# Strassen down-projection for blocks 0 to 15 of the first feed-forward group, with its weight sums split between attention and GpSimd

## The chip, the cores and the metric

The kernel runs on one core of one Trainium2 chip. The metric is the device time of one execution in microseconds; the figure given is the median of three runs. A core has TensorE (PE; its weight loads are listed apart as PEld), VectorE (DVE), ScalarE (ACT), GpSimd (POOL) and SyncE (SP), which here only issues DMAs. Each engine works off its own queue in order and waits on semaphores.

## What is computed

One step of a streaming encoder layer over 2048 prompt tokens and 64 sample tokens (2112 in all), model width 1024, in float32:

```
h  = rmsnorm(x, g1) * (1 + sc1) + sh1          # sc, sh, gt from c @ w_ada
u, q, k, v, o, gates = split(h @ w_in)
mix = concat(pool_mixer(u), mlstm(q, k, v, gates) * sigmoid(o)) @ w_out
x  = x + gt1 * mix
h2 = rmsnorm(x, g2) * (1 + sc2) + sh2
up = h2 @ w_up                                  # 1024 -> 2 * 2816
a, g = split(causal depthwise conv of width 3 over up)
x  = x + gt2 * ((silu(g) * a) @ w_down)         # 2816 -> 1024
y  = rmsnorm(x, g_final)
```

and the states of the pool, the mLSTM and the convolution.

## The kernel before, in words

**Precision.** Every large matmul is done in three passes of `F32R` operands: high x high, high x low, low x high. A weight tile ("unit", 128 x 512) is loaded by SP, ScalarE writes its rounded high part (line 428) and VectorE subtracts that from it for the low part (line 431). `stream` lists all units in the order of use; `pump` loads ahead of use, six or seven units deep.

**Stages.** Attention runs over four groups of 512 tokens (the last has 576). The feed-forward part then runs over three groups of 704 tokens, two column halves of 352 each, and 22 blocks of 128 gated features. `PARTS` (line 33) cuts the blocks of each group into parts. In a part, each block's up-projection (`Pair.products`, line 1720) is done in Strassen's form (Winograd's variant): seven products of 12 matmuls, with sums of the weights (`wsum`, made during attention) and sums of the activations (`Bo`: the seven operands B11, B21, T1 to T4 and B22). Two results make the a and g halves, which go through the convolution, silu and gate.

**The down projection** of a part comes in two forms. *Plain* (`down`, matmuls at line 2230): for each of eight rows of 128 outputs, all blocks of the part, in columns 0 to 448 and 448 to 704; 24 x 2 matmuls per block. *Strassen* (`quad_down`, matmuls at line 2084), for parts of exactly four blocks (`paired`, line 39): the four gated blocks are split into seven operands by `step_2` to `step_7` (ScalarE the high parts, VectorE the low parts and the differences `less`, line 1831), and two `duo`s of 14 half products each, of six matmuls of 352 columns, are added to the rows `x` (line 2053). A quad is held back and done after the first block of the next part. It needs 14 weight units: raw quarters from `w_quad` and sums from `dsum`, eight sets `d` of four matrices, two sets to a quad. `dsum` is made by `quad_sums` (line 1666) in 16 pieces, each a load, four VectorE operations of 128 x 256 and a store.

Before the change, groups two and three have `(0,4) (4,8) (8,12) (12,16) (16,22)`: four quads and one plain part. The first group has `(0,6) (6,12) (12,16) (16,22)`: one quad and three plain parts, because `dsum` is made only while it runs.

**Side work and its order.** In the feed-forward part PE, ACT, DVE and POOL run in the order of the program text. Side work is written as generators in five queues `bg`; `tick(i)` runs the next step of queue i at marked places of the main work, and `drain` runs a queue to its end on the spot. `bg[0]` is ticked twice in each product, `bg[1]` four times a block and after every fourth half product of a quad. `bg[4]` is ticked in attention's projections (line 485), not while `quiet` is set. `quad_sums` runs from `bg[0]` in the first feed-forward group. Ahead of blocks 12 to 15 there, `drain(0)` finishes it and `bg[1]` is set aside.

`prepare` (line 840) makes the next group's `Bo` in the background of `bg[1]`: it normalises rows (line 750), then `sums_of` with `slow=True` makes seven operands for each of four row pairs: ScalarE a high part (line 809), VectorE the low part (line 795) and the sums (line 791), ScalarE's queue the store to `Bd`. `up_sums` (line 874) makes `wsum` in attention: 44 pieces of two loads, four VectorE operations of 128 x 256 (lines 898 to 903) and a store, on `bg[4]` from attention's second group on.

GpSimd's queue in the feed-forward part holds the halo copies of the convolution (`ext_tile`, `conv_scale`, lines 1572 and 1586) and, in the last part of a group, additions of squares (line 2045).

Of the kernel before, what the change touches and what calls it, by code (L numbers as in the profile page):

```python
# [16 lines left out]
P = 128  # L17
# [7 lines left out]
NF = 22  # L25
# [41 lines left out]
def tile_layer(ctx: ExitStack, tc: tile.TileContext, xT, vecs, cst, rst, w_mod, w_ada, w_qkou, w_v, w_pool,  # L67
# [716 lines left out]
    def sums_of(xs, put, slow=False, pin=lambda d: d):  # L784

        H = FH
# [3 lines left out]
        def minus(out, a, b):  # L790
            pin(dve.tensor_tensor(out=out, in0=a, in1=b, op=ALU.subtract))

        def low():
            for nm, src, hi, lo, end in late:
                pin(dve.tensor_tensor(out=lo, in0=src, in1=hi.bitcast(F32), op=ALU.subtract))
# [71 lines left out]
    if True:  # L867
# [6 lines left out]
        def up_sums():  # L874

            def load(f, c):
                w = a1.tile([P, 4, 256], F32, tag="w4", name="w4", bufs=4)
                for i in range(2):
                    tc.keep_in_program_order(nc.sync.dma_start(out=w[:, 2 * i:2 * i + 2, :], in_=w_up[NF * i + f].rearrange(
                        "p (h c) -> p h c", h=2)[:, :, c:c + 256]))  # L880
                return w
            todo = [(f, c) for f in range(NF) for c in (0, 256)]
# [3 lines left out]
            def store():  # L886
                if made:
                    f, c, w = made.pop()
                    pin(nc.sync.dma_start(out=wsum[f, :, :, c:c + 256], in_=w))
# [582 lines left out]
        for o in groups:  # L1472
            drain(1)
            if o.g == 1:
                bg[4].append(up_sums())
# [55 lines left out]
            quiet.append(1)  # L1531
            mix[:NH] = [mx_tile(gi, o) for gi in range(NH)]
# [133 lines left out]
    def quad_sums(ds):  # L1666

        for d in ds:
            for c in (0, 256):
                t = f2.tile([P, 2, FT], F32R, tag="av", name="qs", bufs=AVB)  # L1670
                w = t.bitcast(F32).rearrange("p a t -> p (a t)")[:, :1024].rearrange("p (i c) -> p i c", i=4)
                nc.sync.dma_start(out=w, in_=w_quad[d, :, :, c:c + 256])
                for _ in range(7):
                    yield
                a11, a12, a21, a22 = (w[:, i] for i in range(4))
                dve.tensor_tensor(out=a22, in0=a21, in1=a22, op=ALU.add)
                yield
                dve.tensor_tensor(out=a21, in0=a11, in1=a21, op=ALU.subtract)
                yield
                dve.tensor_tensor(out=a11, in0=a22, in1=a11, op=ALU.subtract)  # L1680
                yield
                dve.tensor_tensor(out=a12, in0=a12, in1=a11, op=ALU.subtract)
                yield
                yield
                nc.sync.dma_start(out=dsum[d, :, :, c:c + 256], in_=w)
                yield
                yield

# [20 lines left out]
    class Pair:  # L1709
# [121 lines left out]
        def less(self, out, a, b):  # L1831
            dve.tensor_tensor(out=out, in0=a, in1=b, op=ALU.subtract)
# [223 lines left out]
    def quad_down(o, quad, cur, done, last=False):  # L2056
# [7 lines left out]
        def duo(d):  # L2064
            units, banks = {}, {}

            def half_product(nm, role, X, op, first=False):
# [20 lines left out]
                tick(1 if len(count) % 4 == 0 else 0)  # L2088
# [74 lines left out]
    for o in fgroups:  # L2163
        Bo = B[o.g]
        held = None
        for pi, part in enumerate(PARTS[o.g]):
# [224 lines left out]
```

## Time and profile before

| what | value |
|---|---|
| median of three runs | 2168.61 us (2168.05 to 2170.31) |
| span of the profiled execution | 2165.8 us |
| PE, DVE, ACT, POOL busy | 2143.9, 1649.8, 1105.2, 265.3 us |
| attention, to the first up-product | 787.1 us |
| first feed-forward group: to its last plain part; that part | 414.7; 47.7 us |
| second group, the same | 405.5; 47.8 us |
| third group, to its last plain part | 401.9 us |

The profile is one execution, taken by the hardware profiler. A row of a window gives its bounds and length, the busy time and the instructions of PE, PEld, DVE, ACT and POOL, the granted TensorE clock, the share of the DMA engines and GB/s. A row of a group gives line, engine, operation, output and inputs with their shapes, the count, then busy time, mean duration in ns, and the idle time of the engine ahead of it with what ended most of that. A row of the timeline or of the chain begins with start and length in us. Busy matmuls are pipelined, so PE's busy time says that it had work, not that it ran at its peak.

### The profile page before, as it was taken

The page shows a single profiled execution, that of the slowest core. Times are in us where ns is not written, and L with a number is a line of the kernel's source. Part 1 is how long each engine was busy: PE and PEld are TensorE (multiplying, and loading weights), DVE is VectorE, ACT ScalarE, POOL GpSimd, SP SyncE. Part 2 cuts the span into 40 slices and gives each one's busy share as a digit, 9 for nine tenths or more (in the row PEclk, how much of TensorE's full clock was granted, in tenths as well). Part 3 has the DMA queues.
Part 4 walks back from the last instruction along what each step waited for, and adds up shares of the span by engine and source line. Part 5 has one row for each costly group of instructions (what it writes and reads, how often), then busy time and mean ns, then how long its engine had stood idle before and what let it go on. Part 6 is the DMA issues. An engine that isn't in the chain of part 4 may idle for free.

```text
span 2165.8 us, 38050 instructions
## 1 busy us (share of the span) xinstructions
PE 2143.9 (99%) x13529; PEld 2038.3 (94%) x13529; DVE 1649.8 (76%) x3060; ACT 1105.2 (51%) x2193; POOL 265.3 (12%) x475
## 2 busy tenths in 40 slices
PE   8999999999999999999999999999999999999998
PEld 7888888888899999999999999999999999999998
DVE  5777679677675778788688768988877597887874
ACT  4554335234333557465556445655655365565554
POOL 0010000001000301010001220100101321111112
PEclk9999999999999999999999999999999999999999
DMA  8987997897799689797768976665668675555542
GB/s 320 331 304 225 325 311 249 292 325 259 247 294 296 207 273 317 241 343 248 229 219 305 360 282 207 228 225 202 219 234 276 221 251 190 171 175 188 172 159 76
DMA packets 297063, 541.09 MB, mean 250 GB/s; under 512 B 25728, under 2 KB 113280, under 8 KB 296872
## 3 DMA queue, kind: packets, MB, share of 16 engines
q1 hardware_dynamic: 286280, 513.44, 70.3%
q10 hardware_dynamic: 10592, 25.20, 3.0%
q8 instruction: 107, 1.75, 0.3%
q14 instruction: 84, 0.69, 0.1%
HBM read 412.56 MB, written 125.98 MB: 249 GB/s over the span
## 4 chain that ended last, share of the span: by engine, by line
PE 89%; DVE 4%; DMA 3%; issue 1%; ACT 1%; SPq 0%; POOL 0%; POOLq 0%; DVEq 0%; ACTq 0%
PE mm L1616 37%; PE mm L495 23%; PE mm L2230 11%; PE mm L2084 10%; PE mm L1155 3%; DVE wt L431 1%; PE m L1345 1%; PE m L1365 1%; PE m L1367 1%; PE m L1330 1%; DMA wt<-dsum 0%; PE mm L1091 0%; DMA qs<-w_quad 0%; DVE tg L1594 0%; DMA raw<-w_up 0%
## 5 line engine op out<-in xcount | busy, mean ns | idle before, releaser
L1616 PE MATMUL mm<-hx,wt 128*128 128x352 f32 x5544 | 886.1, 321 | 2.5 <-DVE wt L431 2.2
L1616 PEld LDWEIGHTS mm<-hx,wt 128*128 128x128 f32 x5544 | 878.3, 188 | 4.9 <-DVE wt L431 4.2
L495 PE MATMUL mm<-hl,wt 128*128 128x512 f32 (+2 forms) x1920 | 385.4, 356 | 0.0
L431 DVE TENSOR_TENSOR wt<-raw,wt 128x512 fp32r<-128x512 f32 (+1 forms) x460 | 310.8, 681 | 79.1 <-ACT wt L428 77.7
L428 ACT ACTIVATE wt<-raw 128x512 fp32r<-128x512 f32 (+1 forms) x460 | 274.7, 604 | 168.0 <-PE mm L495 53.2
L495 PEld LDWEIGHTS mm<-hl,wt 128*128 128x128 f32 x1920 | 314.7, 188 | 47.4 <-issue 4.4
L2084 PE MATMUL mm<-av,wt 128*128 128x352 f32 x1512 | 248.0, 323 | 1.7 <-DVE x L2053 0.7
L2084 PEld LDWEIGHTS mm<-av,wt 128*128 128x128 f32 x1512 | 242.3, 188 | 4.8 <-DVE ea L1625 2.8
L2230 PE MATMUL mm<-av,wt 128*128 128x448 f32 (+1 forms) x1440 | 231.4, 322 | 0.0
L2053 DVE SCALAR_TENSOR_TENSOR x<-mm,MOD,x 128x352 f32<-128x352 f32 (+3 forms) x368 | 171.9, 507 | 77.8 <-PE mm L2230 62.0
L2230 PEld LDWEIGHTS mm<-av,wt 128*128 128x128 f32 x1440 | 220.8, 188 | 9.7
L1664 ACT ACTIVATE mm<-mm 128x352 f32<-128x352 f32 x204 | 91.4, 448 | 238.9 <-PE mm L1616 175.1
L495 PE MATMUL mm<-mx,wt 128*128 128x512 f32 (+1 forms) x960 | 182.6, 352 | 0.0
L495 PEld LDWEIGHTS mm<-mx,wt 128*128 128x128 f32 x960 | 159.3, 188 | 22.5
L1594 DVE SCALAR_TENSOR_TENSOR ta<-ea,V,ta 128x704 f32<-128x704 f32 (+1 forms) x132 | 125.7, 953 | 60.4 <-ACT ta L1589 56.3
L1594 DVE SCALAR_TENSOR_TENSOR tg<-eg,V,tg 128x704 f32<-128x704 f32 (+1 forms) x132 | 125.7, 952 | 49.8 <-ACT tg L1589 47.2
L431 DVE TENSOR_TENSOR wt<-wt 128x512 fp32r<-128x512 f32 x204 | 138.7, 685 | 10.9 <-ACT wt L428 10.7
L428 ACT ACTIVATE wt<-wt 128x512 fp32r<-128x512 f32 x204 | 123.8, 622 | 25.9 <-DMA wt<-wsum 24.7
L1572 POOL COPY ea<-UC 128x2 f32<-128x2 f32 x66 | 35.0, 530 | 529.1 <-DVE ta L1594 418.4
L1812 ACT ACTIVATE tg<-tg 128x704 f32<-128x704 f32 (+1 forms) x66 | 52.5, 796 | 71.3 <-DVE tg L1594 71.3
L1155 PE MATMUL mm<-wt,hl 128*128 128x256 f32 (+1 forms) x576 | 71.2, 284 | 0.0
L1155 PEld LDWEIGHTS mm<-wt,hl 128*128 128x128 f32 x576 | 70.3, 189 | 0.8 <-issue 0.6
(305 smaller groups left out, 2222.7 us busy)
## 6 DMA issues: line engine op xcount, KB each, us to landing
wt<-wsplit SPq DMA_DIRECT2D x132, 512.0 KB, 4.2
raw<-w_up SPq DMA_DIRECT2D x198, 256.0 KB, 4.1
wt<-hl_kept SPq DMA_DIRECT2D x96, 512.0 KB, 5.9
wt<-wsum SPq DMA_DIRECT2D x132, 256.0 KB, 4.9
wsplit<-wt SPq DMA_DIRECT2D x66, 512.0 KB, 5.3
w<-w_up SPq DMA_DIRECT2D x88, 256.0 KB, 4.7
wsum<-w SPq DMA_DIRECT2D x44, 512.0 KB, 5.3
Bd<-fscr ACTq DMA_DIRECT2D x56, 352.0 KB, 3.4
```

The lines of the kernel that those rows point to most:

```text
L428: act.activation(u.w[:, 0, :u.n], u.raw[:, :u.n], AF.Copy)
L431: dve.tensor_tensor(out=u.w[:, 1, :u.n], in0=u.raw[:, :u.n], in1=u.w[:, 0, :u.n].bitcast(F32), op=ALU.subtract)
L495: pe.matmul(ps[bi][:, :hi - lo], U[:, a, k % 4 * P:(k % 4 + 1) * P], mv[k][:, b, lo:hi], start=(at == 0 and pi == 0), stop=(k == order[-1] ...
L1155: pe.matmul(ps[ti][:n, :cols], h[4 * kh + k4][:, b, lo:lo + n], U[:, a, k4 % 2 * cols:(k4 % 2 + 1) * cols], start=(kh == 0 and k4 == 0 and ...
L1572: pool.tensor_copy(ext[:, 0:2], UC[:, f, :])
L1594: dve.scalar_tensor_tensor(out=t[:, :E], in0=ext[:, j:j + E], scalar=wc(j, f), in1=t[:, :E], op0=ALU.mult, op1=ALU.add)
L1616: pe.matmul(bk.t[:, :FH], U[:, a, kc * P:(kc + 1) * P], Bo.at(nm, kc, b), start=(first and kc == 0 and pi == 0), stop=(kc == 3 and pi == 2 ...
L1664: act.activation(to.t[:, :FH], bk.t[:, :FH], AF.Copy)
L1812: act.activation(self.tg[:, :E], self.tg[:, :E], AF.Silu)
L2053: dve.scalar_tensor_tensor(out=x3[n][:, a:b], in0=bk.t[:, a - lo:b - lo], scalar=gt2(n, s), in1=x3[n][:, a:b], op0=ALU.mult, op1=ALU.add)
L2084: pe.matmul(bk.t[:, :FH], U[:, a, c:c + P], quad.put(op, m, b), start=(first and m == 0 and pi == 0), stop=(m == 1 and pi == 2), skip_grou ...
L2230: pe.matmul(bks[i].t[:, :hi - lo], U[:, a, k % 4 * P:(k % 4 + 1) * P], av[k][:, b, lo:hi], start=(k == 0 and (a, b) == PASSES[0]), stop=(k ...
```

## The change

- `PARTS`: the first group gets the parts of the other two, so quads 0 to 2 are added and two plain parts of six blocks go. The drain and the set-aside queue ahead of blocks 12 to 15 go.
- `up_sums` becomes `weight_sums`: after the 44 pieces it makes eight more, of `dsum` sets 0 to 3. It is put on `bg[4]` in the first attention group, ahead of its pooling projections, and takes a piece in 3.5 steps where it took four.
- `quad_sums` makes the other eight pieces (sets 4 to 7), with GpSimd in place of VectorE, in scratch tiles of their own, on `bg[1]` from the first block on, ahead of `prepare`.
- `sums_of(slow=True)`, so `prepare` for groups two and three, makes its low parts and sums on GpSimd.
- `less` is on GpSimd in the first group.
- In the first group a quad ticks `bg[1]` after every third half product.

```diff
-PARTS = (((0, 6), (6, 12), (12, 16), (16, 22)), ((0, 4), (4, 8), (8, 12), (12, 16), (16, 22)),
+PARTS = (((0, 4), (4, 8), (8, 12), (12, 16), (16, 22)), ((0, 4), (4, 8), (8, 12), (12, 16), (16, 22)),
-SUMS = ((6, 7, 0, 1, 2), (3, 4, 5))
...
     def sums_of(xs, put, slow=False, pin=lambda d: d):
+        eng = pool if slow else dve
...
-            pin(dve.tensor_tensor(out=out, in0=a, in1=b, op=ALU.subtract))
+            pin(eng.tensor_tensor(out=out, in0=a, in1=b, op=ALU.subtract))
...
-                pin(dve.tensor_tensor(out=lo, in0=src, in1=hi.bitcast(F32), op=ALU.subtract))
+                pin(eng.tensor_tensor(out=lo, in0=src, in1=hi.bitcast(F32), op=ALU.subtract))
...
-        def up_sums():
+        def weight_sums():
...
+                if f >= NF:
+                    tc.keep_in_program_order(nc.sync.dma_start(out=w, in_=w_quad[f - NF, :, :, c:c + 256]))
+                    return w
...
-            todo = [(f, c) for f in range(NF) for c in (0, 256)]
+            todo = [(f, c) for f in range(NF + QUADS) for c in (0, 256)]
...
-                    pin(nc.sync.dma_start(out=wsum[f, :, :, c:c + 256], in_=w))
+                    to = wsum[f] if f < NF else dsum[f - NF]
+                    pin(nc.sync.dma_start(out=to[:, :, c:c + 256], in_=w))
...
                 yield
-                yield
+                if i % 2:
+                    yield
...
-            if o.g == 1:
-                bg[4].append(up_sums())
...
             quiet.append(1)
+            if o.g == 0:
+                bg[4].append(weight_sums())
...
     def quad_sums(ds):
+        def load(d, c):
+            w = [fscr()[:, :512].rearrange("p (i c) -> p i c", i=2) for _ in range(2)]
+            for i, t in enumerate(w):
+                nc.sync.dma_start(out=t, in_=w_quad[d, :, 2 * i:2 * i + 2, c:c + 256])
+            return w
         for d in ds:
             for c in (0, 256):
...
+                w = load(d, c)
+                yield
+                yield
+                (a11, a12), (a21, a22) = [(t[:, 0], t[:, 1]) for t in w]
+                pool.tensor_tensor(out=a22, in0=a21, in1=a22, op=ALU.add)
+                pool.tensor_tensor(out=a21, in0=a11, in1=a21, op=ALU.subtract)
+                yield
+                pool.tensor_tensor(out=a11, in0=a22, in1=a11, op=ALU.subtract)
+                pool.tensor_tensor(out=a12, in0=a12, in1=a11, op=ALU.subtract)
+                yield
+                for i, t in enumerate(w):
+                    nc.sync.dma_start(out=dsum[d, :, 2 * i:2 * i + 2, c:c + 256], in_=t)
...
         def less(self, out, a, b):
-            dve.tensor_tensor(out=out, in0=a, in1=b, op=ALU.subtract)
+            (pool if self.o.g == 0 else dve).tensor_tensor(out=out, in0=a, in1=b, op=ALU.subtract)
...
-                tick(1 if len(count) % 4 == 0 else 0)
+                tick(1 if len(count) % (4 if o.g else 3) == 0 else 0)
...
-            if quad is not None and o.g == 0:
-                drain(0)
-                aside, bg[1][:] = list(bg[1]), []
...
-                if o.g == 0 and f == 2:
-                    bg[0].append(quad_sums(SUMS[0]))
+                if o.g == 0 and f == 0:
+                    bg[1].append(quad_sums((4, 5, 6, 7)))
                     bg[1].append(prepare(fgroups[1], fscr))
...
-                    if o.g == 0:
-                        bg[0].append(quad_sums(SUMS[1]))
-                        bg[1].extend(aside)
```

More of the change, by code (lines that the diff above doesn't have):

```diff
@@ L1666, in quad_sums @@
     def quad_sums(ds):
+        def load(d, c):
[3 more added lines that the diff above has]
+            return w
         for d in ds:
             for c in (0, 256):
[L1670 to L1682, printed above, removed]
+                w = load(d, c)
                 yield
                 yield
-                nc.sync.dma_start(out=dsum[d, :, :, c:c + 256], in_=w)
+                (a11, a12), (a21, a22) = [(t[:, 0], t[:, 1]) for t in w]
+                pool.tensor_tensor(out=a22, in0=a21, in1=a22, op=ALU.add)
+                pool.tensor_tensor(out=a21, in0=a11, in1=a21, op=ALU.subtract)
                 yield
+                pool.tensor_tensor(out=a11, in0=a22, in1=a11, op=ALU.subtract)
+                pool.tensor_tensor(out=a12, in0=a12, in1=a11, op=ALU.subtract)
                 yield
+                for i, t in enumerate(w):
+                    nc.sync.dma_start(out=dsum[d, :, 2 * i:2 * i + 2, c:c + 256], in_=t)
     def half_tile(nm):
```

## The prediction, made before the changed kernel ran

> **What bounds the kernel now.** I read the page first, for the engines' shares, then the windows of the three feed-forward groups, then the chain, for what a stretch of TensorE work takes, and last the groups by form and the timeline, for prices and for what VectorE and GpSimd do to each other.
>
> ```profile
> span 2165.8 us, 38050 instructions
> PE 2143.9 (99%) x13529; PEld 2038.3 (94%) x13529; DVE 1649.8 (76%) x3060; ACT 1105.2 (51%) x2193; POOL 265.3 (12%) x475
> 787.12:1201.80 414.68, 412.98 (x2596) 407.26 (x2596) 336.33 (x556) 247.40 (x446) 47.29 (x87) 1.00 0.80 275
> 1249.52:1654.98 405.46, 403.45 (x2529) 400.81 (x2529) 333.54 (x540) 240.29 (x446) 44.34 (x89) 1.00 0.67 229
> 1702.73:2104.63 401.90, 401.48 (x2526) 400.29 (x2525) 316.52 (x603) 218.71 (x403) 76.07 (x175) 1.00 0.56 189
> ```
>
> TensorE is busy 99% of the span, so a saving counts where its matmuls leave the path and nothing takes their place. The three windows run from a feed-forward group's first product to its last plain down stage; columns are length, then busy time of PE, PEld, DVE, ACT, POOL. The first group, which the change rewrites, takes 414.68 us; the third, which already runs Strassen in blocks 0 to 15, takes 401.90. VectorE is second: 336.33 of 414.68 us, 81%.
>
> ```profile
> 872.81 41.99 PE mm L2230 x264
> 914.80 78.09 PE mm L1616 x492
> 996.76 1.90 PE mm L1616 x12
> 1111.24 23.05 PE mm L2084 x144
> 1138.14 3.24 DMA Bd<-fscr
> 1149.80 8.46 DMA qs<-w_quad
> ```
>
> From the chain: a plain down matmul (L2230, mean of 448 and 256 columns) costs 41.99/264 = 0.159 us, a Strassen half product's (L2084, 352 columns) 23.05/144 = 0.160 us, and six blocks of up-products 78.09 + 1.90 = 80.0 us, 13.3 per block. So the first group without stalls is 22 x 13.3 + 576 x 0.159 + 168 x 0.160 = 293.3 + 91.6 + 26.9 = 411.8 us. The other 2.9 us are lost near 1138 to 1161 us, where the drain ahead of blocks 12 to 15 issues sums and preparation in a heap and the chain leaves PE for DMAs.
>
> **The change part by part.** *Down product, blocks 0 to 11.* Two plain parts of six go: 2 x 8 rows x 6 blocks x 3 passes x 2 column halves = 576 matmuls, 91.6 us. Three quads come: 3 x 28 half products x 6 = 504 matmuls, 80.7 us. Saved: **10.9 us**. The drain and the set-aside queue go as well: **2.9 us**. The stall-free first group becomes 293.3 + 4 x 26.9 = 400.9 us, close to the third's 401.90.
>
> *VectorE in that group.* Its prices come from the window's groups by form (count | busy, mean ns):
>
> ```profile
> L431 DVE TENSOR_TENSOR wt<-raw,wt 128x512 fp32r<-128x512 f32 x87 | 59.5, 686 | 7.2 <-ACT wt L428 7.2
> L431 DVE TENSOR_TENSOR wt<-raw,wt 128x256 fp32r<-128x256 f32 x16 | 6.7, 417 | 0.0
> L2053 DVE SCALAR_TENSOR_TENSOR x<-mm,MOD,x 128x352 f32<-128x352 f32 x24 | 13.3, 579 | 2.3 <-PE mm L2084 2.2
> L2053 DVE SCALAR_TENSOR_TENSOR x<-mm,MOD,x 128x448 f32<-128x448 f32 x16 | 10.9, 682 | 10.9 <-PE mm L2230 10.9
> L2053 DVE SCALAR_TENSOR_TENSOR x<-mm,MOD,x 128x256 f32<-128x256 f32 x16 | 7.7, 482 | 13.2 <-PE mm L2230 13.2
> L1900 DVE TENSOR_TENSOR av<-tg,av 128x704 fp32r<-128x704 f32 x16 | 14.3, 893 | 3.2 <-ACT av L1895 3.2
> L1828 DVE TENSOR_TENSOR av<-tg,av 128x352 fp32r<-128x352 f32 x6 | 3.1, 522 | 0.3 <-ACT av L1825 0.2
> L1844 DVE TENSOR_TENSOR av<-tg,av 128x704 fp32r<-128x704 f32 x4 | 3.5, 882 | 0.0
> L1832 DVE TENSOR_TENSOR tg<-tg 128x352 f32<-128x352 f32 x8 | 4.0, 523 | 0.1
> L795 DVE TENSOR_TENSOR fscr<-fscr 128x352 fp32r<-128x352 f32 x28 | 14.6, 520 | 2.1 <-ACT fscr L809 2.1
> L791 DVE TENSOR_TENSOR fscr<-fscr 128x352 f32<-128x352 f32 x16 | 8.0, 522 | 0.3
> L1676 DVE TENSOR_TENSOR qs<-qs 128x256 f32<-128x256 f32 x15 | 6.3, 420 | 1.7 <-DMA qs<-w_quad 1.7
> ```
>
> Added: a quad streams 14 weight units, so 42 x 0.686 = 28.8, where two plain parts stream 16 x 0.686 + 16 x 0.417 = 17.6: +11.2. Row additions: 3 x 24 x 0.579 = 41.7 for 16 x 0.682 + 16 x 0.482 = 18.6: +23.1. Splits: 18 x 0.522 + 12 x 0.882 = 20.0 for 12 x 0.893 = 10.7: +9.3. Removed: the old quad's eight differences (L1832) 4.2; the weight sums, 15 of 16 pieces here, 60 x 0.420 = 25.2; the preparation's 28 low parts and 16 differences (L795, L791) 22.9. Net -8.7: VectorE falls to about 328 us of 401, no more loaded than in the second group. ScalarE, 247.40 us of the window, gains some 26 weight copies, 24 bank copies and 18 splits; even at VectorE's 0.7 us for such shapes that is 48 us and under 75% of 401, so I cost it at nothing.
>
> *GpSimd.* It takes what VectorE drops: in the first group 32 sums of 256 columns, 44 preparation operations and 8 pairs x 4 = 32 differences of 352. No 352-wide operation of GpSimd is in the trace; its two-input additions bracket it:
>
> ```profile
> L2045 POOL TENSOR_TENSOR ssum<-ssum,fscr 128x448 f32<-128x448 f32 x4 | 4.6, 1156 | 7.5 <-ACT fscr L2044 7.5
> L2045 POOL TENSOR_TENSOR ssum<-ssum,fscr 128x256 f32<-128x256 f32 x4 | 2.9, 736 | 8.8 <-ACT fscr L2044 8.8
> 1239.63 1.71 POOL L2045 TENSOR_TENSOR ssum<-ssum,fscr 128x704 f32<-128x704 f32 x1 [4.07 <-ACT fscr L2044]
> 1240.04 1.85 DVE L431 TENSOR_TENSOR wt<-raw,wt 128x512 fp32r<-128x512 f32 x1 [1.11 <-ACT wt L428]
> 1221.65 4.09 POOL L2045 TENSOR_TENSOR ssum<-ssum,fscr 128x704 f32<-128x704 f32 x2 [16.20 <-ACT fscr L2044]
> 1224.56 0.68 DVE L2053 SCALAR_TENSOR_TENSOR x<-mm,MOD,x 128x448 f32<-128x448 f32 x1 [0.39 <-PE mm L2230]
> ```
>
> Halfway between 0.736 and 1.156 is 0.946 us. So GpSimd gains 32 x 0.736 + 76 x 0.946 = 95 us on 47 of about 401: a third busy, and alone harmless. That 28 of them write fp32r should cost nothing, since VectorE's L795 and L791 cost the same; at worst I let them take the 1.71 us of a 704-wide one, 21 us more on GpSimd.
>
> The timeline rows carry the real price. The weight subtraction at 1240.04 us, normally 0.686, took 1.85: it began 0.41 us into a GpSimd addition that ran to 1241.34 and ended 0.55 us behind it. So a VectorE operation with two SBUF inputs waits out a GpSimd operation that reads SBUF, all but some 0.15 us. An operation with one input in PSUM does not: the row addition at 1224.56, inside two additions that last to 1225.74, took its usual 0.68. [...]
>
> So each 352-wide operation can hold VectorE for 0.946 - 0.15 = 0.80 us and each 256-wide one for 0.586. Below, the price is zero, where VectorE is idle or reads PSUM, or where a queued VectorE operation follows at once and GpSimd waits. No row shows which of two waiting ones goes first. I take three quarters, nearer the upper end, as the timeline's rows stand there: 0.6 and 0.44.
>
> Where this decides is the middle of the group, from block 4 to block 16 with four quads, 13 x 13.3 + 4 x 26.9 = 281 us:
>
> ```profile
> 1066.27:1092.93 26.66, 26.66 (x170) 26.58 (x169) 23.04 (x35) 18.57 (x34) 4.31 (x8) 1.00 0.74 246
> 1321.14:1347.32 26.18, 26.18 (x163) 26.18 (x164) 24.09 (x44) 13.40 (x27) 1.31 (x2) 1.00 0.56 182
> L750 DVE SCALAR_TENSOR_TENSOR fscr<-fscr,G,rb 128x640 f32<-128x640 f32 x2 | 1.8, 876 | 0.0
> 990.00:1000.00 10.00, 10.00 (x63) 9.70 (x62) 9.35 (x16) 6.63 (x12) 0.63 (x3) 1.00 0.69 233
> ```
>
> The first window is two blocks of the old quad: VectorE 23.04 us, with four differences of about 0.5 that go, so 10.6 per block. The second is a quad of group two, 24.09 with about 3 us of preparation and differences (the L750 row is of that window): 21.3. Preparation leaves VectorE about 15 us of scaling. Together 13 x 10.6 + 4 x 21.3 + 15 = 238 of 281 us. In that stretch fall about half of the sums (16), 40 preparation operations and 26 differences: at my price 16 x 0.44 + 66 x 0.6 = 47 us, VectorE at 285. That is 4 us over, and TensorE must wait for it; with about 1.5 us of small waits, of which the third group shows 1.0 and the second 4.6 over the 400.9: **5.5 us back**. The ends of the group have slack (no second Strassen pair in blocks 0 to 3, plain splits from 16).
>
> *Group two* prepares the third on GpSimd too: 44 operations, VectorE -22.9 and +26 blocked on 333.54 of 405.46: nothing, between -3 and +5.
>
> *Attention.* The generator of weight sums starts in the first group's output projection instead of in group two and makes 52 pieces, not 44: 32 VectorE operations of 0.42, 13 us, and 8 x 1.05 MB of DMA on SP's queue, with a piece now every 3.5 turns. By the code's turns it still ends ahead of the drain that closes attention: eight turns more, and 185 needed where 180 were.
>
> ```profile
> L889 SPq DMA_DIRECT2D wsum<-w x44: 554/562/1103, 241.8 to 737.7; - x44
> 391.63:571.44 179.81, 179.31 (x986) 152.83 (x985) 137.39 (x289) 71.72 (x170) 11.62 (x16) 1.00 0.87 288
> ```
>
> VectorE is at 76% there, the DMA engines at 0.87; 8.4 MB at 288/0.87 = 330 GB/s is 25 us, and the 500 us from the first store of sums to the last leave about 65 free. I take **1 us**, between 0 and 4. The sums that move also take 8.4 MB from the first feed-forward group, which gets 42 units of 256 KB for 16 and 16 half ones, 4.7 MB: less traffic.
>
> ```profile
> L1572 POOL COPY ea<-UC 128x2 f32<-128x2 f32 x66 | 35.0, 530 | 529.1 <-DVE ta L1594 418.4 <-ACT tg L1589 97.5 <-ACT eg L1629 8.6
> ```
>
> *Waits.* GpSimd's new operations stand in its queue ahead of the halo copies (0.5 us each) and behind DMA loads issued two turns earlier, some 6 us at four turns a block; a halo copy that comes late holds up a tap of the convolution on VectorE. Behind a late one wait ScalarE's next high part and its DMA issue, one turn (3 us) later, and SP's stores of the sums, with the weight loads behind them; seven units are in flight, so this costs nothing unless GpSimd falls over 3 us back.
>
> **Sum.** -10.9 - 2.9 + 5.5 + 1 = -7.3 us, 2158.5 of span. The median of 2168.61 is 2.8 above the profiled span: **2161.3 us**. A difference under 0.2%, 4.3 us, cannot be told from none here.
>
> **Rivals.** *The block costs nothing* (VectorE's queue goes first and GpSimd waits): stalls as in the third group, about 1.5: 2157. For it: GpSimd is idle over 60% of the time and most of its results are wanted a block later. Against: L431's 1.85 us.
>
> *VectorE becomes the bound.* Every GpSimd operation holds it for its full length: 16 x 0.586 + 66 x 0.80 = 62 us in the middle, 300 of 281, so 19 us of stall with the small waits near 21; -13.8 + 21 + 1 = +8, **2177**, slower. It decides from a block of about 0.70 us for a 352-wide operation (78 x 0.70 + 238 - 281 + 1.5 = 13, where all of the gain is eaten), and sooner if GpSimd's fp32r writes are long. [...]
>
> *Attention pays.* Its DMA engines are the busiest in the kernel; if each of the eight pieces delays a weight load by 0.9 us, 7 us go there: 2168, no change. Against: the chain there is almost all TensorE.
>
> That the change doesn't do what it says is hard to imagine: the parts list alone sets the quads.
>
> **How the numbers follow.** Forecast 0.44, own range 2158 to 2166; free block 0.20; VectorE bound 0.26; attention 0.10. Faster takes the free block and four fifths of the forecast, 0.55; same the rest of it and attention, 0.19; slower 0.26. The range from 2155 to 2178 leaves out half of the bound case and a little below.
>
> **What would show it.** L2084 with 2016 matmuls and L2230 with 864; the first group's window near 407 us; GpSimd up some 95 us there and 42 in group two; means of L431 above 0.686 wherever GpSimd subtracts. The forecast is wrong if TensorE's waits for VectorE in that window stay under 2 us, or exceed 12, or if the three attention groups grow by more than 3.

## The result, and the profile after

The changed kernel took 2201.2 us (median of 4 runs, 2196.54 to 2204.52), the kernel before beside it 2168.76: 1.0147 times as long, with a 95% interval of 1.0133 to 1.0161. The forecast was 2161.3 with a range to 2178. It is slower by 32 us, beyond the rival that was priced for that side.

First the head of the page, then the windows of the three feed-forward groups, each from the first product to the last plain down stage (columns as before).

```profile
span 2199.9 us, 38134 instructions
PE 2148.5 (98%) x13457; PEld 2038.9 (93%) x13457; DVE 1684.6 (77%) x3000; ACT 1125.2 (51%) x2245; POOL 449.2 (20%) x627
```
```profile
792.60:1234.65 442.05, 415.00 (x2525) 406.95 (x2524) 368.09 (x522) 271.35 (x500) 180.54 (x195) 0.98 0.77 257
1282.30:1689.20 406.90, 404.27 (x2532) 401.61 (x2531) 331.54 (x496) 239.55 (x446) 94.76 (x133) 1.00 0.67 226
1735.30:2139.30 404.00, 403.30 (x2539) 401.81 (x2539) 316.75 (x604) 218.81 (x402) 75.44 (x175) 1.00 0.57 188
```

TensorE issues 13457 - 13529 = -72 matmuls, as forecast. The span is 34.1 us longer, and the windows say where: the first group's main stretch went from 414.68 to 442.05 (+27.4), though its stall-free length, as the prediction worked it out, fell to 400.9; the first product now comes at 792.6 for 787.1 (+5.5); the rest is +1.2. What TensorE waited for in the first group (total us, times, longest) comes next, then what SP's queue waited for between 793 and 975 us.

```profile
PE mm L1621 <- DVE wt L430: 8.2, 8, 1.7
PE mm L2088 <- ACT mm L1669: 6.3, 3, 4.6
PE mm L2088 <- DVE wt L430: 4.5, 4, 1.6
PE mm L2088 <- DVE ea L1630: 4.1, 4, 1.4
PE mm L1621 <- ACT mm L1669: 3.6, 2, 2.9
```
```profile
SPq L1691 <- POOL fscr L1688: 35.3, 8, 5.9
SPq L435 <- DVE wt L430: 19.7, 16, 3.6
```

Two things stand out. VectorE's low parts of the weights (L430, before L431) hold TensorE up twelve times, by at most 1.7 us, and SP's queue stood eight times, for 35.3 us in all, on the store of a weight sum (L1691) that GpSimd had not finished. What that does downstream is seen in the chain just ahead of the longest idle time of TensorE, that of 4.57 us:

```profile
888.81 0.73 POOL fscr L1684
...
891.25 0.73 POOL fscr L1688
...
892.00 0.37 SPq L1691
...
892.42 5.16 DMA wt<-dsum
...
898.14 0.46 ACT mm L1669
...
898.64 1.54 PE mm L2088 x4
```

GpSimd's four operations, from 888.81 on, end at 891.98, the store goes out, and only behind it the load of a weight unit that the quad needs (`wt<-dsum`, issued at 892.42). It lands 5.16 us later, and TensorE starts again at 898.64. SP had issued nothing between 887.62 and 892.00. The wait is put down to ScalarE's bank copy (L1669), but that copy stood in ScalarE's queue behind the high part of this very unit.

The group rows show what VectorE and GpSimd do to each other (count | busy, mean ns | idle time ahead), and the timeline one such meeting:

```profile
L430 DVE TENSOR_TENSOR wt<-raw,wt 128x512 fp32r<-128x512 f32 x89 | 70.8, 800 | 10.6 <-ACT wt L427 10.6
L1848 DVE TENSOR_TENSOR av<-tg,av 128x704 fp32r<-128x704 f32 x16 | 20.9, 1308 | 2.9 <-ACT av L1845 2.9
```
```profile
L1836 POOL TENSOR_TENSOR tg<-tg 128x352 f32<-128x352 f32 x32 | 42.7, 1343 | 31.1 <-DVE tg L1824 22.4 <-DVE av L1832 8.6
L795 POOL TENSOR_TENSOR fscr<-fscr 128x352 fp32r<-128x352 f32 x28 | 34.8, 1241 | 54.5 <-ACT fscr L809 54.5
```
```profile
871.94 1.58 POOL L1836 TENSOR_TENSOR tg<-tg 128x352 f32<-128x352 f32 x1
874.08 0.94 POOL L1836 TENSOR_TENSOR tg<-tg 128x352 f32<-128x352 f32 x1
```
```profile
872.65 1.43 DVE L430 TENSOR_TENSOR wt<-raw,wt 128x512 fp32r<-128x512 f32 x1
874.38 1.39 DVE L1848 TENSOR_TENSOR av<-tg,av 128x704 fp32r<-128x704 f32 x1 [0.30 <-ACT av L1845]
```

The subtraction at 874.38 (L1848; this form, L1844 before, had a mean of 0.882) began inside GpSimd's 0.94 us and ended 0.5 us late; at 871.94 it was GpSimd's turn to be long, 1.58 for 0.94. Both engines pay: L430 has a mean of 0.800 for 0.686 and GpSimd's 352-wide operations 1.24 to 1.34 for 0.94.

### The profile page after: what moved, and what is told of

The parts are those of the page before. It is cut to its first block, busy times and chain, and to the rows that moved or that the text cites. A ratio compares the mean times of both kernels' runs of the same rounds, so it can differ in the third digit from the quotient of the medians.

```text
span 2199.9 us, 38134 instructions
## 1 busy us (share of the span) xinstructions
PE 2148.5 (98%) x13457; PEld 2038.9 (93%) x13457; DVE 1684.6 (77%) x3000; ACT 1125.2 (51%) x2245; POOL 449.2 (20%) x627
## 4 chain that ended last, share of the span: by engine, by line
PE 46%; DVE 8%; DMA 5%; issue 3%; ACT 2%; POOL 1%; SPq 0%; ACTq 0%; DVEq 0%; POOLq 0%
PE mm L1621 28%; PE mm L2088 12%; PE mm L2228 6%; DVE wt L430 2%; DMA wt<-wsum 1%; DVE tg L1599 1%; DMA wsplit<-wt 1%; DMA fscr<-w_quad 1%; ACT tg L1594 1%; DVE tg L1824 1%; DMA wt<-dsum 1%; DMA raw<-w_up 1%; DMA raw<-w_quad 1%; DVE x L2057 0%; DVE ta L1599 0%
## 5 line engine op out<-in xcount | busy, mean ns | idle before, releaser
L430 DVE TENSOR_TENSOR wt<-raw,wt 128x512 fp32r<-128x512 f32 (+2 forms) x446 | 325.1, 734 | 96.2 <-ACT wt L427 94.8
L2088 PE MATMUL mm<-av,wt 128*128 128x352 f32 x2016 | 335.1, 325 | 16.5 <-ACT mm L1669 6.3
L427 ACT ACTIVATE wt<-raw 128x512 fp32r<-128x512 f32 (+2 forms) x446 | 269.7, 610 | 143.5 <-PE mm L2088 41.0
L2057 DVE SCALAR_TENSOR_TENSOR x<-mm,MOD,x 128x352 f32<-128x352 f32 (+5 forms) x408 | 194.1, 515 | 61.1 <-PE mm L2228 38.3
L1669 ACT ACTIVATE mm<-mm 128x352 f32<-128x352 f32 x228 | 102.2, 448 | 247.7 <-PE mm L1621 167.0
L430 DVE TENSOR_TENSOR wt<-wt 128x512 fp32r<-128x512 f32 x228 | 163.6, 726 | 15.6 <-ACT wt L427 15.4
L427 ACT ACTIVATE wt<-wt 128x512 fp32r<-128x512 f32 x228 | 139.0, 622 | 54.2 <-DMA wt<-wsum 29.5
L2228 PE MATMUL mm<-av,wt 128*128 128x448 f32 (+1 forms) x864 | 139.0, 322 | 0.0
L795 POOL TENSOR_TENSOR fscr<-fscr 128x352 fp32r<-128x352 f32 x56 | 67.4, 1203 | 177.7 <-ACT fscr L809 177.7
L1392 POOL TENSOR_TENSOR sf<-sf,half 128x4 f32<-128x4 f32 (+1 forms) x20 | 21.0, 1053 | 268.1 <-DVE sf L266 268.1
```

The source lines that it names most:

```text
L427: act.activation(u.w[:, 0, :u.n], u.raw[:, :u.n], AF.Copy)
L430: dve.tensor_tensor(out=u.w[:, 1, :u.n], in0=u.raw[:, :u.n], in1=u.w[:, 0, :u.n].bitcast(F32), op=ALU.subtract)
L795: pin(eng.tensor_tensor(out=lo, in0=src, in1=hi.bitcast(F32), op=ALU.subtract))
L1669: act.activation(to.t[:, :FH], bk.t[:, :FH], AF.Copy)
L2057: dve.scalar_tensor_tensor(out=x3[n][:, a:b], in0=bk.t[:, a - lo:b - lo], scalar=gt2(n, s), in1=x3[n][:, a:b], op0=ALU.mult, op1=ALU.add)
L2088: pe.matmul(bk.t[:, :FH], U[:, a, c:c + P], quad.put(op, m, b), start=(first and m == 0 and pi == 0), stop=(m == 1 and pi == 2), skip_grou ...
```

## The experiments

Three causes were set against each other. **Q**: stores of sums that wait for GpSimd hold up the weight loads behind them on SP's queue. **L**: GpSimd's reading of SBUF holds VectorE. **D**: the Strassen form itself gives VectorE so much to do in the first group that TensorE loses time well before VectorE is full. Kernels of one batch ran on the same chip. "Main stretch" is the first group's window as above; its stall-free length is 400.9 us with four quads.

| kernel | batch | median us | ratio to before (95%) | main stretch us | VectorE | GpSimd |
|---|---|---|---|---|---|---|
| before | | 2168.76 | | 414.7 | 336.3 | 47.3 |
| after | | 2201.2 | 1.0147 (1.0133 to 1.0161) | 442.05 | 368.1 | 180.5 |
| e1 stores later | 1 | 2185.6 | 1.0078 (1.0063 to 1.0093) | 428.3 | 369.1 | 181.1 |
| e2 sums on VectorE | 1 | 2187.66 | 1.0082 (1.0067 to 1.0097) | 427.5 | 369.6 | 147.1 |
| e3 nothing added to GpSimd | 1 | 2186.16 | 1.0075 (1.0057 to 1.0093) | 430.8 | 377.9 | 49.4 |
| e4 Strassen alone | 1 | 2178.26 | 1.0044 (1.0029 to 1.0059) | 418.8 | 363.0 | 49.3 |
| e5 all sums in attention | 2 | 2182.78 | 1.0066 (1.0051 to 1.0081) | 422.7 | 360.3 | 150.3 |
| e6 before, eight pieces in attention | 2 | 2172.15 | 1.0019 (1.001 to 1.0029) | 417.8 | 329.8 | 46.2 |
| e7 e4 less one tap | 2 | 2162.74 | 0.9973 (0.9963 to 0.9982) | 404.5 | 324.3 | 52.6 |
| e8 e4 with idle GpSimd work | 2 | 2205.54 | 1.0168 (1.0151 to 1.0185) | 445.2 | 397.9 | 145.0 |
| e10 e8 with writes only | 3 | 2177.45 | 1.0038 (1.0024 to 1.0051) | 417.5 | 361.3 | 110.3 |
| e11 one quad more than before | 3 | 2185.4 | 1.0074 (1.0061 to 1.0087) | 435.6 | 360.9 | 46.8 |
| e12 e4 less the preparation | 4 | 2168.78 | 1.0001 (0.9992 to 1.001) | 408.4 | 344.5 | 61.7 |
| e13 before, lighter drain | 4 | 2172.93 | 1.0019 (1.001 to 1.0029) | 414.5 | 334.3 | 47.2 |

Before took 2169.14, 2169.01, 2170.14 and 2168.61 us beside batches 1 to 4. A profiled execution can lie 3.5 us from its kernel's median (e6: 2175.68), so a difference of that size between two single profiles says little. TensorE's clock stood at half for part of some main stretches (last section): 13.7 us of the changed kernel's, 3.4 of e1's, 6.8 of e3's, 17.0 of e8's and 10.2 of e11's, none of the others'.

**e1, the stores later.** Nothing is moved between engines; a store of sums is issued only two turns after its arithmetic, behind the next piece's load.

```diff
...
                 w = load(d, c)
                 yield
                 yield
+                store()
...
                 yield
-                for i, t in enumerate(w):
-                    nc.sync.dma_start(out=dsum[d, :, 2 * i:2 * i + 2, c:c + 256], in_=t)
+                made.append((d, c, w))
...
```

> The changed kernel with one edit: in the first feed-forward group a piece's sums are stored two turns later, behind the next piece's load, so that SyncE no longer stands at a store until GpSimd is done. GpSimd's work is the same. Theory Q (the queue: SyncE waits 35 us at these stores between 793 and 975 us of the changed kernel's trace, and the weight loads wait behind it): most of the 26 us that blocks 0 to 7 lose comes back, 2178 to 2188 us. Theory L (VectorE is held by GpSimd's operations, which are all still there): no change, 2197 to 2204. Theory D (the Strassen form itself asks too much of VectorE): no change, 2197 to 2204.

The window of e1, and the wait that is left of the store's:

```profile
790.30:1218.60 428.30, 411.31 (x2525) 401.85 (x2524) 369.13 (x516) 270.80 (x500) 181.11 (x195) 1.00 0.79 263
```
```profile
SPq L1684 <- POOL fscr L1696: 15.1, 4, 4.6
```

VectorE and GpSimd are as busy as in the changed kernel (369.13 and 181.11 us), and yet the stretch is 13.75 us shorter and the median 15.6 us less. So Q is real. Up to 5 us of the 13.75 came by way of the clock (last section).

**e2 and e3, back to VectorE step by step.** e2 gives the weight sums of the first group back to VectorE; e3 also the preparation's operations and the differences, so that only the four quads and the places of the sums are left of the change. One line of the four of the sums is shown; the last two edits are e3's alone.

```diff
...
-                pool.tensor_tensor(out=a22, in0=a21, in1=a22, op=ALU.add)
+                dve.tensor_tensor(out=a22, in0=a21, in1=a22, op=ALU.add)
...
-        eng = pool if slow else dve
+        eng = dve
...
-            (pool if self.o.g == 0 else dve).tensor_tensor(out=out, in0=a, in1=b, op=ALU.subtract)
+            dve.tensor_tensor(out=out, in0=a, in1=b, op=ALU.subtract)
```

> The changed kernel with the 32 sums of blocks 0 to 7's stretch on VectorE instead of GpSimd (13 us of VectorE), all else the same; the stores then wait for VectorE. Theory L: 32 of 108 GpSimd operations that hold VectorE go, about 0.4 us each, for 0.42 us of its own: little change in VectorE's load, but its results come sooner: 2190 to 2200. Theory Q: the stores come as soon as VectorE has been through its queue, which is sooner than GpSimd: 2182 to 2194. Theory D: VectorE has more to do: 2200 to 2208.

> The changed kernel with all that it gave to GpSimd (sums, the preparation's low parts and sums, the differences) back on VectorE. VectorE then has about 381 us of work for 401 us in the first group, and no GpSimd operation holds it. Theory L: VectorE gets 53 us of work for the 40 us that it was held, but in order and without waiting for GpSimd's longer operations: 2170 to 2185. Theory D: VectorE is the bound and gets more: 2200 to 2215. Theory Q: stores wait for VectorE instead: 2185 to 2195.

Both come out near e1's time, 427.5 and 430.8 us. With the sums on VectorE the stores no longer wait for GpSimd (for VectorE they wait 13.3 us in e2), and the stretch loses about as much as e1's does. With nothing at all added to GpSimd, 29.9 us above 400.9 are still lost: L cannot be the whole of the rest.

**e4, Strassen alone.** All 16 pieces of sums are made in attention, and nothing is added to GpSimd: besides the edits shown, e4 has e3's two of `eng` and `less`.

```diff
...
-            todo = [(f, c) for f in range(NF + QUADS) for c in (0, 256)]
+            todo = [(f, c) for f in range(NF + 2 * QUADS) for c in (0, 256)]
...
-                if i % 2:
-                    yield
...
-                    bg[1].append(quad_sums((4, 5, 6, 7)))
```

> Strassen for blocks 0 to 15 of the first group alone: all 16 pieces of sums are made in attention (a piece every three turns), nothing is given to GpSimd, differences and preparation are on VectorE. VectorE has about 368 of 401 us in the first group, no sums and none of their stores are there. Theories L and Q: the first group runs like the second (405 us for 414.7) and attention pays 6 to 11 us for 16 more pieces: 2164 to 2174. Theory D: the first group still stalls by over 20 us: 2180 to 2195.

The window of e4, the two largest of TensorE's waits in it, and the chain ahead of one quad:

```profile
795.00:1213.80 418.80, 408.06 (x2526) 401.41 (x2525) 362.98 (x591) 272.23 (x500) 49.29 (x87) 1.00 0.74 251
```
```profile
PE mm L2086 <- DVE ea L1628: 5.0, 4, 2.0
PE mm L1619 <- DVE wt L430: 4.8, 9, 1.1
```
```profile
1014.40 1.20 DVE wt L430 x2
...
1017.22 0.96 DVE tg L1597
...
1019.08 0.52 DVE fscr L795
1019.59 1.22 DVE wt L430 x2
...
1020.82 0.32 SPq L435
...
1021.24 6.39 DMA wt<-wsum
...
1029.06 0.52 ACT wt L427
...
1030.35 0.99 ACT tg L1592
...
1031.43 0.96 DVE tg L1597
...
1033.29 0.52 DVE fscr L795
1033.81 0.60 DVE wt L430
```

TensorE loses 17.9 us of 418.8 while VectorE is idle for 55.8. The chain shows how that can be. VectorE works in order, so a weight's low part (L430, the pair at 1019.59) stands behind a tap of the convolution (L1597) and a step of the preparation (L795). SP's queue then holds the store of that split unit (L435, 1020.82) and behind it the next load, which takes 6.39 us. ScalarE, in order too, stands idle for 1.44 us until the load has landed (at 1027.63), so its later work, the start of the next convolution (L1592) included, comes late; behind that stand VectorE's tap, its preparation step and the low part at 1033.81, for which the quad's weight loads wait. This is a ring through the queues of VectorE, SP and ScalarE, and it runs late long before VectorE is full.

The first group has work in this ring that the others don't. It stores 66 split units (L435), which groups two and three load ready made: e4's first group has 208 low parts, 138.9 us of VectorE, its second group 145, 98.0 us. What the place of these stores on SP's queue adds was not tried.

**e5, all sums in attention, the rest on GpSimd.** Only the three edits that are shown for e4.

> Like e4_strassen_alone (all 16 pieces of sums in attention; 2178.3 us there), but the preparation's 44 low parts and sums and the 32 differences are on GpSimd again in the first group. VectorE's own work falls from 363 to about 325 us there. Theory L (a GpSimd operation holds VectorE for about 0.6 us, more than the 0.44 us that VectorE would have needed for it): no gain, 2176 to 2188. Theory D (VectorE's own demand is what stalls TensorE, and GpSimd's operations cost it little): 2164 to 2171.

Against e4, 76 operations of the first group go from VectorE to GpSimd, 39.5 us by VectorE's 0.52, and VectorE's busy time falls by 2.7, from 363.0 to 360.3. The stretch grows by 3.9 us and the median by 4.5 (their batches' before differ by 0.1). That is L's mechanism with its net effect: the moved work comes back as blocked time. Where e3 and e2 show the same step on top of the sums, it goes 3.3 us the other way, so it is worth about nothing, within 4 us. e1 against e5 puts the sums on GpSimd, once the stores are late, at 5.6 us, hardly more than two profiles of one kernel differ by.

**e6, attention's part alone.** The kernel before, with four sets of sums made by the changed generator in attention.

```diff
-SUMS = ((6, 7, 0, 1, 2), (3, 4, 5))
+SUMS = ((6, 7, 4), (5,))
...
             quiet.append(1)
+            if o.g == 0:
+                bg[4].append(weight_sums())
...
```

> The kernel before with one part of the change: the generator of weight sums starts in the first attention group and makes eight pieces more (sets 0 to 3); the other eight are made in the first feed-forward group on VectorE as before (sets 6, 7, 4, then 5). If attention pays for the eight pieces, as the first product's start in the changed kernel and its variants says (790 to 793 us for 787): 2170 to 2174, with some of it back as VectorE has 13 us less in the first group. If that shift was chance: 2166 to 2169.

The eight pieces cost 3.1 us of the median net of what they save later. The window of attention's third group in the changed kernel tells where (the one before stands in the prediction, 179.81 us), and the next row what TensorE waits for there:

```profile
392.80:576.90 184.10, 180.59 (x985) 152.55 (x984) 139.73 (x299) 71.13 (x170) 12.01 (x16) 1.00 0.89 296
```
```profile
PE mm L494 <- DMA wt<-hl_kept: 3.5, 4, 1.5
```

That group goes from 179.8 to 184.1 us, with weight loads that land late. In e4, with 16 pieces in attention, the same window is 187.1 us long, and the fourth group takes 215.7 in all three.

**e7, one tap less.** e4, with the demand on VectorE cut: the kernel leaves out one tap of the convolution in the first group.

```diff
+        if o.g == 0 and j == 0:
+            return
         dve.scalar_tensor_tensor(out=t[:, :E], in0=ext[:, j:j + E]
...
```

> e4_strassen_alone with one of the two VectorE taps of the convolution left out in the first group (44 operations of 0.95 us, so its output leaves out the oldest row of the window there): about 38 us less for VectorE, 325 of 401 us, as much as it has in the second group, and nothing else changed. Theory D: the first group's 18 us of stalls shrink to the second group's 4, 2162 to 2168. Theories L and Q have nothing to act on in this kernel and give no change, 2176 to 2180.

With VectorE at 324.3 us the stretch takes 404.5, 3.6 above stall-free: 14.3 us come back for 38.7 us of VectorE's work. That is what D expected. ScalarE (269.0 us) and the DMA engines (0.78) are as busy as in e4 (272.2 and 0.74), so their load is not what cost e4 its 17.9 us.

**e12, the preparation left out.** e7 shortens a chain that each block waits for; this run takes away background work instead: the kernel leaves out the low parts and sums of the next groups' activations. The low parts are edited like the line shown.

```diff
...
-            pin(eng.tensor_tensor(out=out, in0=a, in1=b, op=ALU.subtract))
+            pin(pool.memset(out, 0.0) if slow else dve.tensor_tensor(out=out, in0=a, in1=b, op=ALU.subtract))
```

> e4 (Strassen in the first group, no sums and no added GpSimd work there) with the preparation's 44 VectorE operations per group replaced by writes of zero on GpSimd, so that the kernel leaves out the low parts and sums of the activations of groups two and three. e7 took VectorE work out of the convolution, which is part of the chain that a block waits for; this takes out background work that no block waits for. VectorE falls by 44 x 0.52 = 23 us, from 363 to about 340 of the first group's window. If TensorE lost its 18 us in e4 because VectorE as a whole has too much to do (theory D): window 407 to 411 us for e4's 418.8, 2166 to 2170 us for e4's 2178.3. If it lost them because the convolution's chain of dependent steps is too long beside a quad, whatever else VectorE does: window 415 to 419 us, 2174 to 2178.

```profile
793.10:1201.50 408.40, 405.00 (x2524) 401.36 (x2524) 344.46 (x546) 271.94 (x499) 61.71 (x131) 1.00 0.77 257
```

408.4 us, as D said: 18.5 us less on VectorE, 10.4 less lost. So the convolution's chain alone isn't the cause. Taps and preparation steps both stand ahead of low parts in VectorE's queue, so the two runs don't part VectorE's load from its order.

**e8 and e10, GpSimd beside e4.** e8 adds one subtraction on a tile that nobody else uses, four times a block in the first group; e10 makes of each two writes of a constant.

```diff
...
+            pool.tensor_tensor(out=idle, in0=idle, in1=idle, op=ALU.subtract)
```
```diff
...
+            for _ in range(2):
+                pool.memset(idle, 0.0)
```

> e4_strassen_alone with 88 idle GpSimd subtractions of 128x352 on a tile of their own in the first group, four a block, that nobody waits for: the price of a GpSimd operation beside VectorE alone. Theory L at 0.6 us each: 53 us more for VectorE, which has 363 of 419 already, so 2205 to 2230. If VectorE's queue goes first and GpSimd waits: 2178 to 2184.

> This is e8 with each of the 88 idle subtractions of GpSimd (two inputs read from SBUF) replaced by two writes of a constant to the same 128x352 tile, so that GpSimd is about as busy and reads nothing. e4, the same kernel without GpSimd's idle work, took 2178.3 us, with VectorE at 363 us of the first group; e8 took 2205.5, with 397.9. If it is the shared reading of SBUF that holds VectorE: 2177 to 2182 us, VectorE 361 to 367 us in the window, the weight subtractions (L430) no longer than in e4. If any work of GpSimd holds VectorE, or GpSimd's queue holds up the convolution's halo copies: 2190 us or more, with VectorE above 375 us in the first case and its busy time unchanged in the second.

Group rows of e8, then of e10, with the same VectorE group and the idle work in each:

```profile
L1597 DVE SCALAR_TENSOR_TENSOR tg<-eg,V,tg 128x704 f32<-128x704 f32 x42 | 50.7, 1207 | 10.4 <-ACT tg L1592 9.6
...
L1696 POOL TENSOR_TENSOR idle<-idle 128x352 f32<-128x352 f32 x84 | 94.4, 1124 | 3.3
```
```profile
L1597 DVE SCALAR_TENSOR_TENSOR tg<-eg,V,tg 128x704 f32<-128x704 f32 x42 | 39.9, 951 | 13.6 <-ACT tg L1592 9.7 <-POOL idle L1697 3.1
...
L1697 POOL MEMSET idle<- 128x352 f32 x168 | 65.8, 392 | 7.2
```

In e8 VectorE's busy time grows by 34.9 us with no work added to it, 0.40 for each of 88 subtractions, and the stretch by 26.4. Up to 8.5 us of that are the clock's, so one subtraction costs the stretch 0.20 to 0.30 us. In e10 GpSimd does 65.8 us of writes and nothing moves: 361.3 us of VectorE, 417.5 of stretch, 2177.45 us. So of the two it is the operation that reads SBUF, not the one that only writes it, that holds VectorE here, and L is shown as a mechanism. It shows on the 118 weight subtractions (L430, `wt<-wt`), whose two inputs are in SBUF: their mean is 749 ns in e8, 685 in e4 and 684 in e10. The 96 row additions, which read one input from PSUM, have 575, 581 and 577.

**e11, half of it.** The kernel before with one quad more: plain parts of blocks 0 to 3 and 4 to 7, quads from block 8, all sums on VectorE from block 0 on.

```diff
...
-    return part[1] - part[0] == NQ
+    return part[1] - part[0] == NQ and (g > 0 or part[0] >= 8)
...
-SUMS = ((6, 7, 0, 1, 2), (3, 4, 5))
+SUMS = (4, 5, 6, 7, 0, 1, 2, 3)
...
```

> The kernel before with one quad more in the first feed-forward group instead of three: plain parts of blocks 0 to 3 and 4 to 7, quads from 8 to 11 and 12 to 15; all weight sums stay on VectorE in this group, from its first block on, and the drain goes. Stall-free the group is 293.3 + 480 x 0.159 + 336 x 0.160 = 423.4 - the 6 blocks of the last plain part counted in both, that is 293.3 + 384 x 0.159 + 336 x 0.160 = 408.1 us, 3.7 less than the old 411.8. VectorE's demand, by the rows of before: two plain parts of four 16 x 0.686 + 18.6 + 8 x 0.893 = 36.7 and a quad 30.2 in place of 46.9, so 336 + 20 = 356 of 408 us. If TensorE loses only where VectorE's demand is over the time (as the prediction took it): about 409 to 411 us, 2163 to 2165. If it loses already from the chains of dependent work when VectorE is above some 85% (theory D; e4 lost 18 us at 363 of 401, before 3 at 336 of 412, e7 4 at 324 of 401): about 10 us lost, 417 to 419 us, 2170 to 2173.

Both expectations failed, 435.6 us, 27.5 above the stall-free 408.1. Another cause came in, of which TensorE's longest wait, in the first plain part of four, is a piece.

```profile
PE mm L2222 <- ACT av L1892: 4.3, 1, 4.3
```

Ahead of the last block's gate there is plain work of two blocks only, where a part of six has four, and the last pair's convolution is not done in that time. Behind this wait the clock stood at half for 6.8 us, and for 3.4 later. With the sums crowded in, the DMA engines were at 0.92 and 1.00 of their time ahead of the two plain down stages, and at 0.71 and 0.80 in the stretches with these. Most of the 27.5 us is not traced, and the run tells nothing about D.

**e13, a lighter drain.** The kernel before, with two pieces of sums moved behind the quad.

```diff
-SUMS = ((6, 7, 0, 1, 2), (3, 4, 5))
+SUMS = ((6, 7, 0, 1), (2, 3, 4, 5))
```

> The kernel before, with four sets of weight sums made ahead of blocks 12 to 15 and four after the quad, where it had five and three, so that the drain has two pieces less to issue in a heap. The prediction took 2.9 us of the first group's 414.7 for the drain's cost and counted them as gained. If that is so, 1.5 to 2.9 us go: window 411.8 to 413.2, 2165.7 to 2167.2 us. If they are VectorE's demand of the group, which this doesn't change: window 414 to 416, 2168 to 2170.

414.5 us: the 2.9 us above stall-free stay, so they weren't the drain's, or not by way of its length. The median is 4.3 us above before, and the stretch from the last plain part to group two's first quad takes 119.8 us for 116.4: the moved pieces are paid there.

None of the runs that keep all of the computation beats the kernel before.

## Why the prediction was wrong

The span was to be 2158.5 and was 2199.9, 41.4 us more: 35.6 in the first group's main stretch (406.4 forecast, 442.05 measured), 4.5 in attention, 1.3 in the rest.

*The matmuls* were right: 72 fewer, and e7's 404.5 us for the same matmuls come near the 400.9 worked out. *The drain's 2.9 us* were counted as gained without a test; e13 says a lighter drain gains none of it.

*VectorE's own demand* was right: 328 us forecast. e4's 363.0 less the 76 operations that the change takes away, 39.5, is 323.5. *The price of a GpSimd operation* was right in kind and too high in size: 368.1 - 323.5 = 44.6 us over 108 operations is 0.41 each, where 0.6 and 0.44 were taken; e8 measures 0.40. GpSimd itself grew by 133 us, not 95, since the block works both ways.

*The step that failed* is the sentence "That is 4 us over, and TensorE must wait for it". It lets TensorE lose only what VectorE's demand has over the time. The runs give another curve for the same stall-free 400.9 us. The last column is what a half clock can have added at most, half of the time that it lasted:

| VectorE busy us | TensorE's loss us | from | of it clock, at most |
|---|---|---|---|
| 316.5 | 1.0 | before, third group | 0 |
| 324.3 | 3.6 | e7 | 0 |
| 333.5 | 4.6 | before, second group | 0 |
| 344.5 | 7.5 | e12 | 0 |
| 363.0 | 17.9 | e4 | 0 |
| 377.9 | 29.9 | e3 | 3.4 |
| 397.9 | 44.3 | e8 | 8.5 |

At no point is VectorE above 400.9, and the loss is up to 44 us. The two rows of the kernel before were in the prediction, and were put down there as "small waits". A further microsecond on VectorE costs TensorE 0.2 between e7 and e12, 0.56 from there to e4, and 0.7 to 0.8 beyond, or 0.5 to 0.6 with the clock's share taken off. The rows are not one experiment: groups two and three are without the stores of split units, and e3 has stores of sums that wait for VectorE. This term was +5.5 in the sum; in e1, which has the change's load and only 15.1 us of waits on SP's queue, it was 27.4, of which the table gives some 22 at 369.1 us. Step by step the loss is 17.9 us with the four quads (e4), 21.8 with preparation and differences on GpSimd (e5), 27.4 with the sums there too (e1) and 41.15 with their stores in the way.

*The second failure* is "so this costs nothing unless GpSimd falls over 3 us back", of SP's stores. They waited 35.3 us, up to 5.9 at once, and e1 prices what hung behind them at 13.75 us of the stretch. Some 5 us of that came by way of the clock (below).

*Attention* was to cost 1 us, between 0 and 4; its third group grew by 4.3. The DMA engines' free time, 65 us over the whole of attention, was no cover in the one group where they were at 0.87. The whole, 5.5 us to the first product, is nearer the 7 us of the rival *Attention pays*, and beyond the 3 us that the prediction named as a sign of being wrong.

*Group two* was right: 406.90 for 405.46.

Of the rivals, *VectorE becomes the bound* had the right engine, and a price of +8 that its own rule held down: it let TensorE lose nothing until VectorE was full. What stays open is where the other 5 us of e1 go: to the clock (1.7 at most), to the waits that are left on SP's queue, or to GpSimd's reads at the wrong moment. They are hardly more than two profiles of one kernel differ by. That the table's losses come by the ring of loads and low parts rests on chains such as e4's; no run changed the depth of the prefetch or moved the stores of split units.

## What to carry to other kernels

An engine that works in order and stands in the ring of the prefetch cost the bound engine time here from about 80% load on (3.6 us at 324.3 of 400.9, e7), so price added work by the loss that stages of the same structure show at their load, not by what exceeds the time. Look at every queue that a changed step's stores stand in: a store that waited for a slow engine, here for up to 5.9 us, held every load behind it, and issuing it two turns later won 13.75 us of the stretch and cost none that was seen. Two-input work given to GpSimd came back here as blocked time on VectorE, 0.40 us for each operation of 352 columns in e8, so it relieved VectorE by little: in e5 by 2.7 us for 39.5 moved.

## What was not expected of the hardware

TensorE's granted clock fell to half, 0.50, in the middle of the work. Windows of e8 come first, two pairs and one without a fall behind it, then two of the changed kernel on the same grid, then its second fall (the share before the last two columns is the granted clock):

```profile
845.79:849.20 3.41, 1.39 (x9) 1.10 (x7) 3.41 (x5) 0.86 (x3) 2.66 (x3) 1.00 0.37 130
849.20:852.61 3.41, 3.41 (x12) 3.41 (x13) 2.24 (x3) 1.17 (x2) 1.69 (x2) 0.50 0.74 210
...
1129.09:1132.50 3.41, 1.84 (x11) 1.27 (x10) 3.13 (x5) 2.72 (x7) 0.51 (x1) 1.00 0.20 74
1132.50:1135.91 3.41, 3.41 (x13) 3.41 (x12) 3.41 (x6) 1.96 (x5) 1.29 (x2) 0.50 0.94 307
1006.20:1009.61 3.41, 1.95 (x13) 1.66 (x12) 3.38 (x6) 2.10 (x4) 0.79 (x2) 1.00 0.38 129
```
```profile
799.00:802.41 3.41, 2.80 (x9) 2.80 (x10) 1.99 (x3) 2.08 (x5) 0.00 (x0) 0.50 0.93 313
945.77:949.18 3.41, 1.78 (x10) 1.48 (x11) 3.41 (x4) 2.08 (x5) 1.45 (x1) 1.00 0.87 305
```
```profile
892.00:898.64 6.64, 2.07 (x12) 1.78 (x13) 3.46 (x7) 1.41 (x4) 0.69 (x2) 0.95 0.82 202
898.64:904.80 6.16, 6.16 (x21) 6.16 (x22) 3.16 (x6) 2.86 (x6) 0.00 (x0) 0.50 0.74 253
904.80:911.00 6.20, 6.20 (x41) 6.20 (x40) 4.65 (x9) 0.63 (x1) 0.00 (x0) 1.00 0.64 226
```

Behind a stretch in which TensorE was busy for only 1.39 or 1.84 of 3.41 us, the clock stood at 0.50 for the next 3.41; behind one with 1.95 it stayed at 1.00. Of the five falls of e8 (849.2, 876.5, 948.2, 1040.3, 1132.5 us) the last lies 283.3 us, 83 times 3.413, behind the first, the others 8, 29 and 56 times, so these falls lie on a grid. The changed kernel's two lie 29 times 3.413 us apart, 98.99 us. No busy time parts the windows with a fall behind them from those without: grid windows with 1.82, 1.78 and 1.76 us in the changed kernel (at 874.09, 945.77 and 1119.85 us) brought none. TensorE is busy all through e8's falls, and each lasts one window. In the changed kernel's two falls, at 799.0 and 898.0, it is busy for only 2.80 and 2.76 us of the first window, and a second one follows, 6.8 us in all.

In the second of these, 21 matmuls took 6.16 us where the next 41 took 6.20, so the two cost the changed kernel up to 7 us, while e1 has one fall of 3.4, and some 5 of the 13.75 us that e1 wins back are the clock's. The rest is not: the changed kernel's quickest execution has the mean clock of e1's profiled one, 0.998, and took 2196.54 us for 2185.22.

In e8 a window more than half busy, 1.84 of 3.41 us, stood ahead of a fall, so no wait as long as a window was needed there. That such short stalls are the cause was not tested.
